# Five edits to the order and placement of work around a saturated TensorE in a two-layer retention and gMLP kernel

## The chip, the cores and the metric

The kernel runs on one core of a Trainium2 chip. A core has five engines that run side by side, each with its own instruction stream: TensorE (PE in the profile; PEld is its weight load), VectorE (DVE), ScalarE (ACT), GpSimd (POOL) and SyncE (SP). They work on tiles in on-chip memory (SBUF) and on the banks in which TensorE accumulates (PSUM); DMA queues, fed here by SP (loads, and the stores of the result) and by POOL (spills), move data to and from DRAM. The metric is the device time of one execution in microseconds.

## The reference

A latent stream x (512 tokens, 1024 features) and a context of 256 tokens pass through two layers, each behind an RMSNorm whose scale, shift and output gate come from a conditioning vector ("ada"), and then through a last RMSNorm. All is float32.

```
# layer 0: retention, 4 heads, q and k of 256, v of 512 features, both directions
q, k, v, z = split(h @ w_in)            # q and k with rotary positions
o = retention(q, k, v, log_g)           # scores (q k^T) times a decay matrix, times v; context first
o = o * rsqrt(mean(o * o) + eps)        # per token and head
x = x + gate * ((o * silu(z)) @ w_out)

# layer 1: gMLP, width 2048, 8 groups, chunks of 128 tokens
u, v, z = split(h @ w_in)
v = (v - mean(v)) * rsqrt(mean((v - mean(v))**2) + eps) * vnorm_g
mixed = einsum('gij,bnjgc->bnigc', w_s, v) + b_s
x = x + gate * ((u * mixed * silu(z)) @ w_out)
return rmsnorm(x, final_g)
```

## The kernel before, in words

**Products.** A float32 operand is split into a rounded high part and the rest (`split`: a cast on ScalarE, then a subtraction on VectorE), and each product is three matmuls (`mm3`). Big products are done as a scheme of seven half-size products in place of eight (`Product`, with the items B11, T1, T2, B21, T3, B22, T4 of one "quad"). For an item whose name begins with T, VectorE first subtracts two weight blocks (raw), then ScalarE casts and VectorE subtracts (hl), and TensorE runs 24 matmuls of 256 columns. The class `Stream` (its one instance is `Q`) holds the list of items and of weight loads; `Q.get` hands out an item's split tile and prepares two items ahead. Four hl buffers exist, and 11 small tiles ("t2") for everything of 128x512.

**Layer 0.** After the projections, `attend(h)` runs one head: twice three score steps (hf is the half of the 512 queries, j the pair of key blocks). A score step is 24 matmuls into a "tm" bank of PSUM, then pf (VectorE, times the decay), ph (cast, ScalarE) and pl (subtraction, VectorE). `pv`, two steps behind, multiplies by v into two "ps" banks. After the third pv of a half, `finish` norms it (ScalarE: squares into ss, a root, with a load of its function table; VectorE: reciprocal) and gates it (VectorE: two gt). `flip` transposes gt on TensorE and splits it into og. `project_out` multiplies by the output weights and adds to acc, the residual, which is loaded during head 0's scores. Beside the heads run the loads and splits of the next head's q, k (`load_qk`) and v, and in the background four "ada" pieces (bg) for the next layer's scale, shift and gate.

**Layer 1.** At the end of `project_out` of head 3, `rms(hf)` spreads the roots of a half's norm over the partitions with two tiny matmuls, into a bank of the pool "ps" (6 banks; "tm" has 2). v comes first (28 items): its blocks get their statistics (bn_stats) and are spilled to DRAM (vt). Then for i in 0 to 7, seven items of u and z; `load_vt` fetches v's block i+1 and normalises it; after B22 the spatial mix (16 small matmuls) follows, and `gate_f` gates two blocks of features: Silu on ScalarE, then on VectorE v times scale plus bias (ya, 128x512), times u (two of 128x256), times silu(z), and the split into y. Every second i, `out1(p)` multiplies four feature blocks by the output weights, in two halves hf of the columns; `drain` and `final` add up, norm and store.

**What sets the order.** Helper objects `pe`, `act`, `dve` (class `Queue`, line 54, so nearly all rows of the profile carry L54) issue the instructions. A scheduler places each engine's instructions by the program's text order and by what each waits for; `kept` pins an engine to the text order, `pinned` ties an instruction to the one before it, and `fence()` holds back all later ones of that engine until the one last issued. TensorE is kept throughout. Loads wait in SP's order, and a load waits for its slot (a tag such as "rope" or "w3") to come free.

Of the kernel before, what the change touches and what calls it, by code (L numbers as in the profile page):

```python
# [10 lines left out]
ALU = mybir.AluOpType  # L11
# [56 lines left out]
def hybrid_kernel(ctx, tc, xT_d, cT_d, cv_d, sv_d, rows_d, ada0_d, adag_d, w_d, rope_d, dec_d, ws_d, id_d, out_d):  # L68
# [181 lines left out]
    for q in QUADS[3:]:  # L250
        Q.quad(q, SINGLE)
        for u in RAWS:
            Q.load((q, u), W, 1, parts_of(q, u))
    PROJECTED = len(Q.items)
    def place_at(tag):
        return lambda: st([P, 2, 1024], tag, F32R, name="hl_e")
# [506 lines left out]
    def background():  # L763
        for i in range(4):
            a = None
            for a in ada_piece(i, *(("g1", ("g2", "g3")) if i < 3 else ("oA22", ("w2", "w3")))):
                if a is None:
                    yield
            yield
            if i == 0:  # L770
                yield from columns(a, gate0)
                dve.tensor_tensor(gate0, gate0, gateb0, ALU.add)
            elif i == 1:
                yield from columns(a, sh1)
                dve.tensor_tensor(sh1, sh1, adab1[:, 0, :], ALU.add)
                dve.tensor_tensor(shs, sh1[:, 0:4], sh1[:, 4:8], ALU.add)
            elif i == 2:
                yield from columns(a, gs1)
                dve.tensor_tensor(gs1, gs1, adab1[:, 1, :], ALU.add)
                dve.scalar_tensor_tensor(gs1, gs1, 1.0, g1, ALU.add, ALU.mult)  # L780
            else:
                gb = st([P, D], "g1", name="gateb1")
                load(gb, rows_d[0:1, :].partition_broadcast(P))
                yield
                for j in range(2):
                    pr = pt(tag="tm")
# [49 lines left out]
        dve.tensor_tensor(l, f32(l), f32(h), ALU.subtract)  # L836

    def load_qk(h):
        tags = ("s0", "s1", "s2", "s3", "rope") if h % 2 == 0 else ("w4", "w5", "g2", "g3", "w6")
        srcs = (k_d[h][0], q_d[h][0], k_d[h][1], kc_d[h], q_d[h][1])  # L840
        t = []
        for tag, src in zip(tags, srcs):
            t.append(st([P, 2, 2, HS], tag, F32R, name="qk"))
            load(f32(t[-1][:, 1]).rearrange("p a b -> p (a b)"), src)
            if len(t) % 2:
                yield
        for x in t:
            halves(x)
            yield
        qk[h] = (t[1], t[4]), (t[0], t[2]), t[3]  # L850
        yield
# [77 lines left out]
    def attend(h, qs, vs):  # L929
        q, k, kc = qk.pop(h)  # L930
        v, z = vv.pop(h)
        dt = dts[h]
        og = [st([P, 2, 4, HS], tag, F32R, name="og") for tag in ("oS3", "oS4")]
        steps = [(hf, j) for hf in range(2) for j in range(0, NK, 2)]
        ph, po, pend = {}, {}, []

        def key(j):
            return (k[j // 2], j % 2) if j < NT else (kc, j - NT)

        def score(hf, j):  # L940

            p = pt(tag="tm")
            for o in range(2):
                src, jj = key(j + 1 - o)
                for m in range(2):
                    l = (src[:, 0, m, jj * P:jj * P + P], src[:, 1, m, jj * P:jj * P + P])
                    mm3(p[:, o * HS:o * HS + HS], l, (q[hf][:, 0, m, :], q[hf][:, 1, m, :]), m == 0, m == 1)
            j1 = j + 1
            s0 = hf * HS - P * j1 + P * (NT - 1) if j < NT else XW + hf * HS - P * (j1 - NT) + P * (NC_T - 1)
            base = dt[:, s0:s0 + HS]  # L950
            both = bass.AP(base.tensor, base.offset, [base.ap[0], (P, 2), (1, HS)])
            two = lambda x: x.rearrange("p (o t) -> p o t", o=2)
            a = t2("pf")
            dve.scalar_tensor_tensor(two(a), two(p), 1.0 / 16.0, both, ALU.mult, ALU.mult)
            hl = t2("ph", dt=F32R), t2("pl", dt=F32R)
            split(hl, a)
            ph[hf, j] = hl

        def pv(hf, j):
# [12 lines left out]
        def finish(hf):  # L972
            ss = st([P, 2], "ss", bufs=2)
            for t in range(2):
                act.activation(t2("junk"), po[hf][t], AF.Square, accum_out=ss[:, t:t + 1])
            act.activation(ss, ss, AF.Sqrt, bias=eps, scale=1.0 / 512)
            dve.reciprocal(ss, ss)
            gts = []
            for t in range(2):
                g = t2("gt")  # L980
                dve.scalar_tensor_tensor(g, po[hf][t], ss[:, t:t + 1], z[:, 2 * hf + t, :], ALU.mult, ALU.mult)
                gts.append(g)
            pend.append((hf, gts))

        def flip():
            hf, gts = pend.pop(0)
            for fp in range(2):
                pq = pt()
                for b in range(2):
                    for t in range(2):  # L990
                        o = b * HS + t * P
                        pe.transpose(pq[:, o:o + P], gts[t][:, (2 * fp + b) * P:(2 * fp + b) * P + P], ident)
                src = pq.rearrange("p (b t) -> p b t", b=2)
                split((og[hf][:, 0, 2 * fp:2 * fp + 2, :], og[hf][:, 1, 2 * fp:2 * fp + 2, :]), src)

        LAG = 2
        wo = load_wo(h)
        for i in range(len(steps) + LAG):
            if i < len(steps):
                score(*steps[i])  # L1000
            if i >= LAG:
                pv(*steps[i - LAG])
            aside(qs)
            if i > 4:
                aside(vs)
            if i == len(steps):
                flip()
            if (h, i) == (0, 2):
                for c in range(4):
                    load(acc[:, 2 * c:2 * c + 2, :], xT_d[:, 2 * c:2 * c + 2, :])  # L1010
            if i < 5:
                aside(wo)
            if i in (3, 5, 6):
                step()
        return og, flip

    def project_out(ws, og, flip, parts, then=None, between=None, prepare=None):
# [72 lines left out]
        dve.reciprocal(s[:, 1, :], s[:, 1, :])  # L1090

    def rms(hf):
        pr = pt((P, HS))
        for i in range(2):
            mm(pr[:, i * P:i * P + P], sums[hf][:, 1, i:i + 1].to_broadcast([P, P]), ident, start=True, stop=True)
        rs = st([P, HS], "rs1", name="rs1")
# [114 lines left out]
    def out1(p):  # L1211
        for hf in range(2):
            ws = [Q.get() for _ in range(2)]
            pr = {}
            if p == 3 and hf == 0:
                seq = [(t, k) for ks in ((0, 1, 3), (2,)) for t in range(NT) for k in ks]
            else:
                seq = [(t, k) for t in range(NT) for k in range(4)]
            ends = (2,) if p == 3 and hf == 0 else (3,)
            for t, k in seq:  # L1220
                if k == 0:
                    pr[t] = pt()
                y = yf(4 * p + k)
# [1 line left out]
                mm3(pr[t], (y[:, 0, t * P:t * P + P], y[:, 1, t * P:t * P + P]), (w[:, 0, :], w[:, 1, :]), k == 0, k in ends)  # L1225
                if k in ends:
                    drain(p, t, hf, pr.pop(t))

    def drain(p, t, hf, pr):
        h = slice(hf * 512, hf * 512 + 512)  # L1230
# [15 lines left out]
    def final(t, hf, s, h):  # L1246
# [14 lines left out]
        act.activation(o[:, 512:], o[:, 512:], AF.Copy, scale=ss[:, 1:2])  # L1261
        load(rows[:, 512:], o[:, 512:])

    vts = {}

    def load_vt(i):
        vts[i] = []
        for th in range(2):
            v = t2("vt", (P, 2, HS))
            load(v, vt_d[i][:, 2 * th:2 * th + 2, :])  # L1270
            for t in range(2):
                n = 2 * th + t
                dve.tensor_scalar(v[:, t, :], v[:, t, :], mv[:, n, 0:1], rv[:, n:n + 1], ALU.subtract, ALU.mult)
            vts[i].append(v)

    def gate_f(f, pm, mine):

# [13 lines left out]
        split((y[:, 0, :], y[:, 1, :]), a)  # L1291

    load_vt(0)
    for i in range(UZ):
        got, pms = {}, {}
        prod = Product(features, got.__setitem__)
        for name in SINGLE:
            prod.run(name, Q.get())
            if name == "T2" and i < UZ - 1:
                load_vt(i + 1)  # L1300
            if name == "B22":
                for s in range(2):
                    pm = pms[s] = pt()
                    for n in range(NT):
                        mm(pm[:, n * P:n * P + P], vts[i][n // 2][:, n % 2, s * P:s * P + P], wsT[:, i * P:i * P + P], start=True, stop=True)
                gate_f(2 * i + 1, pms[1], {0: got["12"], 1: got["22"]})
        gate_f(2 * i, pms[0], {0: got["11"], 1: got["21"]})
        if i and i % 2 == 0:
            out1(i // 2 - 1)
    out1(3)  # L1310
# [110 lines left out]
```

## Time and profile before

| | us |
|---|---|
| median of three runs | 913.14 (909.51 to 913.16) |
| profiled execution | 911.76 |
| its span (first to last instruction) | 910.0 |
| busy: TensorE, VectorE, ScalarE | 886.6, 722.4, 445.5 |
| mean granted clock of TensorE | 0.997 |

How to read the rows: "start us, us, engine line op out<-in" is a group of instructions on one engine, xN their number; "[1.40 <-DVE pf L54]" says how long the engine stood idle ahead of it and which instruction ended the wait. Times count from the span's start. A row "PE pst L54 <- DVE hl L54: 3.7, 4, 1.6" gives the total of such waits, their number and the longest. In rows of groups, "| 11.5, 411 |" is the busy time in us and the mean length of one in ns. A window's row has the stretch, its length, and for each engine its busy time and number of instructions, then the clock granted to TensorE, the DMA share and GB/s.

### The profile page before, as it was taken

The numbers are of one execution on the slowest core, as the hardware profiler recorded it, in microseconds if no ns is written. First come the engines' busy times: TensorE is split into PE (matmuls) and PEld (weight loads), VectorE is DVE, ScalarE is ACT, GpSimd is POOL, SyncE is SP. The second block draws the span as 40 slices with busy tenths as digits, with TensorE's granted clock in tenths as the row PEclk, the third lists the DMA queues.
The fourth block names the chain that finished last, engine by engine and source line by source line (L and its number), as shares of the span: only waits on it lengthen the run. The fifth ranks groups of instructions, "written<-read, shape, count | busy, mean of one in ns | idle before, by whom it ended". The sixth has DMA issues, their size and how long they took to land.

```text
span 910.0 us, 16953 instructions
## 1 busy us (share of the span) xinstructions
PE 886.6 (97%) x6872; PEld 840.4 (92%) x6872; DVE 722.4 (79%) x1024; ACT 445.5 (49%) x683; POOL 51.5 (6%) x88
## 2 busy tenths in 40 slices
PE   8999999999999999999999999999999999999987
PEld 6899999999999998998989798999999899899885
DVE  3689978698789866888666759999899479679985
ACT  5565644434545436626362548744546445244244
POOL 0001211101102010000000001111000000000000
PEclk9999999999999999999999999999999999999999
DMA  9943968556667377758163611626335035037102
GB/s 334 389 136 111 308 200 255 163 183 223 211 207 241 107 254 251 257 164 282 43 194 107 200 37 66 200 102 220 129 116 185 24 116 185 24 117 253 49 24 93
DMA packets 76782, 153.81 MB, mean 169 GB/s; under 512 B 7840, under 2 KB 34592, under 8 KB 76704
## 3 DMA queue, kind: packets, MB, share of 16 engines
q1 hardware_dynamic: 69840, 130.70, 44.5%
q0 software_dynamic: 6720, 22.03, 6.3%
q8 instruction: 54, 0.88, 0.4%
q14 instruction: 24, 0.20, 0.1%
q10 hardware_dynamic: 144, 0.01, 0.0%
HBM read 128.58 MB, written 24.12 MB: 168 GB/s over the span
## 4 chain that ended last, share of the span: by engine, by line
PE 61%; DVE 20%; DMA 7%; ACT 5%; issue 5%; SPq 1%; DVEq 0%; ACTq 0%
PE pst L54 61%; DVE hl L54 5%; DMA raw<-in_w_dram 4%; DVE raw L54 4%; DVE ya L54 2%; ACT hl L54 2%; DVE o L54 2%; DMA vt<-vt 2%; SPq L128 1%; DMA acc<-in_xT_dram 1%; DVE pf L54 1%; DMA xq<-in_xT_dram 1%; DVE snap L54 1%; DVE ada_a L54 1%; ACT junk L54 1%
## 5 line engine op out<-in xcount | busy, mean ns | idle before, releaser
L54 DVE TENSOR_TENSOR hl<-raw,hl 128x1024 fp32r<-128x1024 f32 x195 | 236.7, 1222 | 65.5 <-ACT hl L54 64.8
L54 ACT CAST hl<-raw 128x1024 fp32r<-128x1024 f32 x195 | 202.7, 1049 | 140.9 <-DVE raw L54 71.1
L54 PE MATMUL pst<-oS,hl 128*128 128x256 f32 x1104 | 135.6, 280 | 4.3 <-DVE hl L54 3.7
L54 PEld LDWEIGHTS pst<-oS,hl 128*128 128x128 f32 x1104 | 131.4, 188 | 6.6 <-ACT ya L54 3.6
L54 PE MATMUL pst<-hl,oS 128*128 128x256 f32 x1152 | 137.3, 279 | 0.1
L54 PEld LDWEIGHTS pst<-hl,oS 128*128 128x128 f32 x1152 | 135.6, 188 | 1.2 <-ACT snap L54 0.8
L54 PE MATMUL pst<-oA,hl 128*128 128x256 f32 x936 | 118.1, 281 | 0.2
L54 PEld LDWEIGHTS pst<-oA,hl 128*128 128x128 f32 x936 | 112.6, 188 | 2.6 <-DVE raw L54 0.8
L54 DVE TENSOR_TENSOR raw<-raw 128x1024 f32<-128x1024 f32 x92 | 111.5, 1221 | 0.8
L54 PE MATMUL pst<-hl,oA 128*128 128x256 f32 x816 | 99.4, 280 | 0.1
L54 ACT COPY snap<-pst 128x512 f32<-128x512 f32 x92 | 53.9, 586 | 89.4 <-PE pst L54 89.1
L54 PEld LDWEIGHTS pst<-hl,oA 128*128 128x128 f32 x816 | 96.9, 188 | 0.4 <-issue 0.3
L54 PE MATMUL pst<-og,hl 128*128 128x256 f32 x768 | 93.1, 281 | 0.0
L54 PEld LDWEIGHTS pst<-og,hl 128*128 128x128 f32 x768 | 91.2, 188 | 1.0 <-issue 0.5
L54 PE MATMUL pst<-hl,ya 128*128 128x512 f32 x288 | 69.6, 394 | 2.4 <-DVE ya L54 2.4
L54 PEld LDWEIGHTS pst<-hl,ya 128*128 128x128 f32 x288 | 53.9, 188 | 14.7 <-DVE ya L54 2.9
L54 PE MATMUL pst<-v,ph 128*128 128x512 f32 x192 | 60.9, 399 | 0.0
L54 DVE TENSOR_TENSOR snap<-pst,snap 128x512 f32<-128x512 f32 x69 | 47.4, 687 | 4.1 <-PE pst L54 3.9
L54 ACT CAST ph<-pf 128x512 fp32r<-128x512 f32 x24 | 14.9, 621 | 70.9 <-DVE pf L54 68.5
L54 PE MATMUL pst<-hl,hc 128*128 128x256 f32 x384 | 47.5, 279 | 0.0
L54 PEld LDWEIGHTS pst<-hl,hc 128*128 128x128 f32 x384 | 45.9, 188 | 0.0
L54 PEld LDWEIGHTS pst<-v,ph 128*128 128x128 f32 x192 | 36.7, 191 | 7.7
(172 smaller groups left out, 971.8 us busy)
## 6 DMA issues: line engine op xcount, KB each, us to landing
raw<-in_w_dram SPq DMA_DIRECT2D x224, 256.0 KB, 4.5
bg<-in_adag_dram SPq DMA_DIRECT2D x32, 512.0 KB, 4.4
ada_w<-in_ada_dram SPq DMA_DIRECT2D x16, 512.0 KB, 9.0
raw<-in_w_dram SPq DMA_DIRECT2D x16, 512.0 KB, 4.4
bg<-in_dec_dram SPq DMA_DIRECT2D x12, 512.0 KB, 4.3
v<-snap POOLq DMA_DIRECT2D x16, 256.0 KB, 5.1
z<-snap POOLq DMA_DIRECT2D x16, 256.0 KB, 4.7
v<-v SPq DMA_DIRECT2D x8, 512.0 KB, 4.2
```

The lines of the kernel that those rows point to most:

```text
L54: made = op(*args, **kw)
L128: nc.sync.dma_start(dst, src)
```

## The change

1. **q slot.** The last q tile of heads 0 and 2 is loaded into slot "w3" in place of "rope"; the last projection quad leaves "w3" out of its slots, and ada piece 3 uses "rope" in its place.
2. **Gating and last scores.** `finish` ends with the root. Reciprocal and gt move to `gated()`, called after the next score step (and at the loop's end); after the split of the last score step ScalarE and VectorE get a fence.
3. **Spread roots.** `rms` takes a "tm" bank.
4. **v.** `load_vt` only loads (after T1, was T2); `norm_vt` (after T4) normalises by ScalarE, as Identity with bias -mean times root and scale root.
5. **Gating in layer 1.** `gate_f` is put in a list `owed` and issued by `settle()` after the next `Q.get`, behind a fence on VectorE.
6. **The last product.** `out1(3)` for the first half takes features 0 and 1 of all token tiles, then 3, then 2; the last token tile of the second half is done in two halves of 256 columns, each drained by `last`, and the last store is issued from ScalarE's queue.

```diff
-            Q.load((q, u), W, 1, parts_of(q, u))
+            Q.load((q, u), W if q != QUADS[-1] else [w for w in W if w != "w3"], 1, parts_of(q, u))
...
-            for a in ada_piece(i, *(("g1", ("g2", "g3")) if i < 3 else ("oA22", ("w2", "w3")))):
+            for a in ada_piece(i, *(("g1", ("g2", "g3")) if i < 3 else ("oA22", ("w2", "rope")))):
...
-        tags = ("s0", "s1", "s2", "s3", "rope") if h % 2 == 0 else ("w4", "w5", "g2", "g3", "w6")
+        tags = ("s0", "s1", "s2", "s3", "w3") if h % 2 == 0 else ("w4", "w5", "g2", "g3", "w6")
...
             split(hl, a)
+            if (hf, j) == steps[-1]:
+                act.fence()
+                dve.fence()
...
             act.activation(ss, ss, AF.Sqrt, bias=eps, scale=1.0 / 512)
-            dve.reciprocal(ss, ss)
...
+            rest.append((hf, ss))
+
+        def gated():
+            while rest:
+                hf, ss = rest.pop(0)
+                dve.reciprocal(ss, ss)
...
                 score(*steps[i])
+            gated()
             if i >= LAG:
                 pv(*steps[i - LAG])
...
-        pr = pt((P, HS))
+        pr = pt((P, HS), tag="tm")
...
             ws = [Q.get() for _ in range(2)]
             pr = {}
+            settle()
             if p == 3 and hf == 0:
-                seq = [(t, k) for ks in ((0, 1, 3), (2,)) for t in range(NT) for k in ks]
+                seq = [(t, k) for ks in ((0, 1), (3,), (2,)) for t in range(NT) for k in ks]
...
+            if (p, hf) == (3, 1):
+                t = NT - 1
+                for c in range(2):
+                    pq = pt((P, HS))
+                    for k in range(4):
...
+                        mm3(pq, (y[:, 0, t * P:t * P + P], y[:, 1, t * P:t * P + P]), (w[:, 0, :], w[:, 1, :]), k == 0, k == 3)
+                    last(t, c, pq)
...
+    def last(t, c, pq):
+
+        h = slice(512 + c * HS, 512 + c * HS + HS)
+        s = o1[t][:, h]
+        dve.tensor_tensor(s, pq, s, ALU.add)
+        ss, o = ends[t]
+        act.activation(t2("junk1", (P, HS)), s, AF.Square, accum_out=ss[:, 1:2])
+        dve.tensor_tensor(o[:, h], s, fg[:, h], ALU.mult)
+        if c == 0:
+            dve.scalar_tensor_tensor(ss[:, 0:1], ss[:, 1:2], 1.0 / D, ss[:, 0:1], ALU.mult, ALU.add)
+            return
...
+        nc.scalar.dma_start(rows[:, 512:], o[:, 512:])
...
-            for t in range(2):
-                n = 2 * th + t
-                dve.tensor_scalar(v[:, t, :], v[:, t, :], mv[:, n, 0:1], rv[:, n:n + 1], ALU.subtract, ALU.mult)
             vts[i].append(v)
+
+    nb = st([P, NT], "nb")
+    dve.scalar_tensor_tensor(nb, mv[:, :, 0], -1.0, rv, ALU.mult, ALU.mult)
+
+    def norm_vt(i):
+        for n in range(NT):
+            v = vts[i][n // 2][:, n % 2, :]
+            act.activation(v, v, AF.Identity, bias=nb[:, n:n + 1], scale=rv[:, n:n + 1])
+
+    owed = []
+
+    def settle():
+        if owed:
+            dve.fence()
+        while owed:
+            owed.pop(0)()
...
-            prod.run(name, Q.get())
-            if name == "T2" and i < UZ - 1:
-                load_vt(i + 1)
+            w = Q.get()
+            settle()
+            prod.run(name, w)
+            if i < UZ - 1:
+                if name == "T1":
+                    load_vt(i + 1)
+                if name == "T4":
+                    norm_vt(i + 1)
...
-                gate_f(2 * i + 1, pms[1], {0: got["12"], 1: got["22"]})
-        gate_f(2 * i, pms[0], {0: got["11"], 1: got["21"]})
+                owed.append(lambda f=2 * i + 1, pm=pms[1], mine={0: got["12"], 1: got["22"]}: gate_f(f, pm, mine))
+        owed.append(lambda f=2 * i, pm=pms[0], mine={0: got["11"], 1: got["21"]}: gate_f(f, pm, mine))
+        if i == UZ - 1:
+            settle()
```

What this does to the engines' instructions, at three places.

On SP, at the end of layer 0's projections and the start of head 0 (qk<-q_156 is head 0's last q tile, bg the first raw block of an ada piece, acc the residual):

```order
 L128 DMA qk<-k_165 128x512
-L128 DMA bg<-in_adag_dram 128x1024
+L128 DMA qk<-q_156 128x512
 L128 DMA v<-v_175 128x1024
 L128 DMA bg<-in_dec_dram 128x1024
```

```order
 L128 DMA raw<-in_w_dram 128x1024
-L128 DMA acc<-in_xT_dram 128x1024
-L128 DMA qk<-q_156 128x512
-L128 DMA acc<-in_xT_dram 128x1024 x3
+L128 DMA acc<-in_xT_dram 128x1024 x4
+L128 DMA bg<-in_adag_dram 128x1024
```

The q tile has moved up, out of the residual's loads, and the bg block has moved down behind them.

On VectorE, around the last score step of the first half of head 3 (hl_e is the first split of layer 1, raw a weight difference for it, og the split behind the flip):

```order
 L54 TENSOR_TENSOR pl<-pf,ph 128x512
+L54 SCALAR_TENSOR_TENSOR pf<-pst,dt 128x512
+L54 TENSOR_TENSOR hl<-raw,hl 128x1024
+L54 TENSOR_TENSOR pl<-pf,ph 128x512
+L54 RECIPROCAL ss<-ss 128x2
 L54 TENSOR_TENSOR hl_e<-raw,hl_e 128x1024
-L54 TENSOR_TENSOR raw<-raw 128x1024 x2
-L54 RECIPROCAL ss<-ss 128x2
 L54 SCALAR_TENSOR_TENSOR gt<-pst,ss,z 128x512 x2
-L54 TENSOR_TENSOR hl<-raw,hl 128x1024
-L54 SCALAR_TENSOR_TENSOR pf<-pst,dt 128x512
-L54 TENSOR_TENSOR pl<-pf,ph 128x512
```

The last pf and pl, and the split hl between them, have moved ahead of the gating, and one of the two raw that stood ahead of it now follows the next og.

On VectorE in layer 1, where the blocks of u1 are gated while the items of u2 are prepared. Before:

```order
L54 TENSOR_TENSOR raw<-raw 128x1024 x2
L54 TENSOR_TENSOR snap<-pst,snap 128x512
L54 TENSOR_TENSOR hl<-raw,hl 128x1024
L54 SCALAR_TENSOR_TENSOR ya<-pst,sv,bsb 128x512 x2
L54 TENSOR_TENSOR ya<-snap,ya 128x256 x3
L54 TENSOR_TENSOR ya<-ya,yz 128x512
L54 TENSOR_TENSOR ya<-pst,ya 128x256
L54 TENSOR_TENSOR raw<-raw 128x1024
L54 TENSOR_TENSOR ya<-ya 128x512
L54 TENSOR_TENSOR ya<-ya,yz 128x512
L54 TENSOR_TENSOR hl<-raw,hl 128x1024
```

Now:

```order
L54 TENSOR_TENSOR snap<-pst,snap 128x512
L54 TENSOR_TENSOR raw<-raw 128x1024
L54 SCALAR_TENSOR_TENSOR ya<-pst,sv,bsb 128x512
L54 TENSOR_TENSOR ya<-snap,ya 128x256 x2
L54 TENSOR_TENSOR hl<-raw,hl 128x1024
L54 TENSOR_TENSOR ya<-ya,yz 128x512
L54 SCALAR_TENSOR_TENSOR ya<-pst,sv,bsb 128x512
L54 TENSOR_TENSOR hl<-raw,hl 128x1024
L54 TENSOR_TENSOR ya<-ya 128x512
L54 TENSOR_TENSOR ya<-snap,ya 128x256
L54 TENSOR_TENSOR ya<-pst,ya 128x256
```

Before, the split of item T2 (the last hl above) came behind both gates; now it comes behind the first three instructions of one, and the next split behind two more.

More of the change, by code (lines that the diff above doesn't have):

```diff
@@ L934, in attend @@
         steps = [(hf, j) for hf in range(2) for j in range(0, NK, 2)]
-        ph, po, pend = {}, {}, []
+        ph, po, pend, rest = {}, {}, [], []
         def key(j):
@@ L976, in finish @@
             act.activation(ss, ss, AF.Sqrt, bias=eps, scale=1.0 / 512)
-            dve.reciprocal(ss, ss)
-            gts = []
-            for t in range(2):
[L980 to L983, printed above, removed]
+            rest.append((hf, ss))
[3 more added lines that the diff above has]
+                dve.reciprocal(ss, ss)
+                gts = []
+                for t in range(2):
+                    g = t2("gt")
+                    dve.scalar_tensor_tensor(g, po[hf][t], ss[:, t:t + 1], z[:, 2 * hf + t, :], ALU.mult, ALU.mult)
+                    gts.append(g)
+                pend.append((hf, gts))
         def flip():
@@ L1014, in attend @@
                 step()
+        gated()
         return og, flip
@@ L1220, in out1 @@
             for t, k in seq:
+                if (p, hf, t) == (3, 1, NT - 1):
+                    continue
                 if k == 0:
@@ L1227, in out1 @@
                     drain(p, t, hf, pr.pop(t))
+            if (p, hf) == (3, 1):
[3 more added lines that the diff above has]
+                    for k in range(4):
+                        y = yf(4 * p + k)
+                        o = k % 2 * 512 + c * HS
+                        w = ws[k // 2][:, :, o:o + HS]
+                        mm3(pq, (y[:, 0, t * P:t * P + P], y[:, 1, t * P:t * P + P]), (w[:, 0, :], w[:, 1, :]), k == 0, k == 3)
+                    last(t, c, pq)
     def drain(p, t, hf, pr):
@@ L1262, in final @@
         load(rows[:, 512:], o[:, 512:])
+    def last(t, c, pq):
[8 more added lines that the diff above has]
+            return
+        rows = out_d[t * P:t * P + P, :]
+        act.activation(ss[:, 1:2], ss[:, 1:2], AF.Sqrt, bias=ss[:, 0:1], scale=1.0 / D)
+        dve.reciprocal(ss[:, 1:2], ss[:, 1:2])
+        dve.tensor_scalar(o[:, 0:512], o[:, 0:512], ss[:, 1:2], None, ALU.mult)
+        load(rows[:, 0:512], o[:, 0:512])
+        act.activation(o[:, 512:], o[:, 512:], AF.Copy, scale=ss[:, 1:2])
+        nc.scalar.dma_start(rows[:, 512:], o[:, 512:])
     vts = {}
@@ L1270, in load_vt @@
             load(v, vt_d[i][:, 2 * th:2 * th + 2, :])
-            for t in range(2):
-                n = 2 * th + t
-                dve.tensor_scalar(v[:, t, :], v[:, t, :], mv[:, n, 0:1], rv[:, n:n + 1], ALU.subtract, ALU.mult)
             vts[i].append(v)
+    nb = st([P, NT], "nb")
[10 more added lines that the diff above has]
+            owed.pop(0)()
     def gate_f(f, pm, mine):
@@ L1293, in hybrid_kernel @@
     load_vt(0)
+    norm_vt(0)
     for i in range(UZ):
```

## Prediction

> **What bounds the kernel.** I read the page's busy table first, then the waits of TensorE, then the rows around each wait.
>
> ```profile
> span 910.0 us, 16953 instructions
> PE 886.6 (97%) x6872; PEld 840.4 (92%) x6872; DVE 722.4 (79%) x1024; ACT 445.5 (49%) x683; POOL 51.5 (6%) x88
> PE pst L54 <- DVE hl L54: 3.7, 4, 1.6
> PE pst L54 <- DVE pl L54: 3.1, 2, 2.1
> PE pst L54 <- DVE ya L54: 2.4, 1, 2.4
> PE pst L54 <- DVE pf L54: 1.4, 1, 1.4
> PE pst L54 <- ACT xs L54: 1.2, 1, 1.2
> ```
>
> TensorE is busy for 886.6 of 910.0 us, so at most 23.4 us can be won without removing matmuls, and this change removes none. The waits (us in total, times, longest) that it touches add up to 3.7 + 3.1 + 2.4 + 1.4 + 1.2 = 11.8 us in nine places. Everything else is startup, the store at the end, or small. So the sum goes place by place, and what VectorE or ScalarE gain elsewhere counts for nothing.
>
> A wait costs a little more than its idle time, because the end of the last matmul before it is modelled:
>
> ```profile
> 878.84 1.56 PE L54 MATMUL pst<-hl,ya 128*128 128x512 f32 x6
> 882.83 3.48 PE L54 MATMUL pst<-hl,ya 128*128 128x512 f32 x14 [2.43 <-DVE ya L54]
> 882.08 1.29 DVE L54 TENSOR_TENSOR ya<-ya 128x512 fp32r<-128x512 f32 x2
> ```
>
> Fourteen take 3.48 us and six 1.56, so one more costs 1.92/8 = 0.24. The six from 878.84 would let the next start at 880.28; it starts at 882.83, and 2.55 us are lost where 2.43 are shown. I add 0.13 to each wait.
>
> **The change, part by part.**
>
> **The q slot.** Head 0's scores begin late:
>
> ```profile
> 306.68 0.33 SPq L128 DMA_DIRECT2D bg<-in_adag_dram  x1
> 335.78 0.33 SPq L128 DMA_DIRECT2D qk<-q  x1
> 343.49 0.62 ACT L54 CAST qk<-qk 128x512 fp32r<-128x512 f32 x1 [3.54 <-DMA qk<-q]
> 346.75 0.69 DVE L54 SCALAR_TENSOR_TENSOR pf<-pst,dt 128x512 f32<-128x512 f32 x1
> 347.49 1.68 PE L54 MATMUL pst<-qk 128*128 128x256 f32 x12 [1.40 <-DVE pf L54]
> ```
>
> ScalarE stands 3.54 us for the last q tile, issued on SP's queue at 335.78 between the residual (acc) loads; the v splits queue behind it, and the first pf ends at 347.44. In the order of after, this load stands in the place of the bg load of 306.68, some 29 us earlier, and its cast and subtraction lie inside the projection. ScalarE's 3.54 us go; pf then starts some 2 us earlier and TensorE no longer waits: **-1.5 us** (1.40 + 0.13). The bg load moves behind the four acc loads; its reader is background work off TensorE's path. Bounds: 0, if v's splits come as late as before, and -1.8.
>
> **Gating behind the last scores.** Today VectorE gates first, then does pf and pl of the last score step; now the gating (reciprocal and two gt, 0.16 + 1.41 us by rows below) stands behind pl. So the last score-times-v product (pv) no longer waits for pl, but the transposes (flip) ahead of it wait for gt.
>
> ```profile
> 367.76 0.69 DVE L54 TENSOR_TENSOR pl<-pf,ph 128x512 fp32r<-128x512 f32 x1 [0.69 <-ACT ph L54]
> 367.36 1.03 PE L54 MATMUL pst<-ident,gt 128*128 128x128 f32 x8
> 368.50 0.50 PE L54 MATMUL pst<-v,pl 128*128 128x512 f32 x1
> 418.88 0.50 PE L54 MATMUL pst<-v,pl 128*128 128x512 f32 x1 [0.95 <-DVE pl L54]
> ```
>
> In heads 0 to 2 VectorE does the same pieces in another order; the one saving is the 0.69 us that it stands for ph, now filled by splits. The chain that ended with pl at 368.45 now ends with gt at 367.76; the flip takes 1.03 us more, so pv starts at about 368.8 against 368.50. Head 1 goes the same way (from 418.88 to 419.2). I take **+1.05 us** for the three; bounds 0 (all splits hidden earlier) and +3 (nothing filled, and the flip exposed each time).
>
> Head 3 is different:
>
> ```profile
> 512.45 1.05 ACT L54 CAST hl_e<-raw 128x1024 fp32r<-128x1024 f32 x1 [1.44 <-DMA raw<-in_w_dram]
> 513.40 0.59 ACT L54 ACTIVATE junk<-pst 128x512 f32<-128x512 f32 x1
> 516.17 1.03 ACT L54 CAST hl<-raw 128x1024 fp32r<-128x1024 f32 x1
> 511.58 1.57 PE L54 MATMUL pst<-qk 128*128 128x256 f32 x12
> 517.38 1.41 DVE L54 SCALAR_TENSOR_TENSOR gt<-pst,ss,z 128x512 f32<-128x512 f32 x2
> 518.49 1.34 PE L54 MATMUL pst<-ident,gt 128*128 128x128 f32 x8
> 521.96 0.50 PE L54 MATMUL pst<-v,pl 128*128 128x512 f32 x1 [2.12 <-DVE pl L54]
> 522.00:526.00 4.00, 4.00 (x12) 0.64 0.40 130
> ```
>
> Layer 1's first split (hl_e) waits 1.44 us for a load, and the squares for the norm queue behind it on ScalarE; the new fence puts hl_e behind ph. The stretch from the squares to the end of hl's cast (513.40 to 517.20) can then start where the pv ahead of the last scores (511.58) ends, at about 511.2: hl's cast ends at 515.0, ph's (0.6) at 515.6, hl's subtraction (1.22) at 516.2, and pl (0.69) at 516.9. Reciprocal (0.16), hl_e's subtraction (1.23) and gt (1.41) bring 519.5 with their overlaps, the flip (1.0) 520.5, against 521.96: **-1.5 us**. And from 518.49 to 521.96, 3.47 us, TensorE did transposes only; in the window behind it (its columns: length, PE busy, granted clock, DMA share, GB/s) the clock is 0.64, which costs 4.00 x 0.36 = 1.4 us. The new stretch is 2.0 us. After the 2.43 us wait at 882.83 matmuls go at their full 0.24 us, so I take the drop as gone: **-1.4 us**; bounds -1.4 and 0.
>
> The Trainium skill ("TensorE: Matmul & The Clock Gate", Part 1) has the clock halved after an idle window of about 3.4 us that runs freely, and (Part 4) does not count transposes as activity. The rows put the limit between 2.43 and 3.47 us, which agrees; by its figure the sum would stay as it is, but its "HAM oscillation" speaks against a change that adds short waits around transposes: see the third rival.
>
> **The bank of the spread roots.**
>
> ```profile
> 560.20 0.16 DVE L54 RECIPROCAL sums<-sums 128x2 f32<-128x2 f32 x1
> 561.80 0.71 PE L54 MATMUL pst<-ident,sums 128*128 128x128 f32 x4 [1.16 <-ACT xs L54]
> 550.00:600.00 50.00, 48.60 (x408) 47.96 (x409) 49.27 (x71) 37.67 (x63) 6.46 (x12) 1.00 0.44 148
> ```
>
> The roots are ready at 560.36, but TensorE waits until 561.80 for ScalarE to free a "ps" bank (xs). With a "tm" bank it waits for the roots only: 1.16 + 0.13 less some 0.1 gives **-1.2 us**. VectorE is busy for 49.27 of these 50 us, so the time may come back as a wait for hl: bounds -1.5 and 0.
>
> **v normalised by ScalarE, gating deferred.** The four waits for hl all lie in layer 1. The longest:
>
> ```profile
> DVE vt L54 <- DMA vt<-vt: 11.0, 10, 2.0
> L54 DVE TENSOR_SCALAR vt<-vt,mv,rv 128x256 f32<-128x256 f32 x32 | 11.5, 411 | 11.1 <-DMA vt<-vt 11.0
> L54 ACT ACTIVATE f<-f,sh,gs 128x256 f32<-128x256 f32 x16 | 8.3, 592 | 1.1 <-DVE f L54 1.1
> 679.06 1.22 DVE L54 TENSOR_TENSOR hl<-raw,hl 128x1024 fp32r<-128x1024 f32 x1
> 685.84 1.23 DVE L54 TENSOR_TENSOR hl<-raw,hl 128x1024 fp32r<-128x1024 f32 x1
> 682.63 2.99 PE L54 MATMUL pst<-oS,hl 128*128 128x256 f32 x24
> 687.21 1.06 PE L54 MATMUL pst<-oS,hl 128*128 128x256 f32 x7 [1.60 <-DVE hl L54]
> ```
>
> TensorE wants the next item at about 685.5, when the 24 matmuls end; VectorE turns to its subtraction at 685.84, having done both gates since 680.2. In the new order raw comes first (1.22), then one gate's first three pieces (some 1.5), then hl (1.22): ready at about 684.0 at the latest, 1.5 us ahead, and 1.4 us more are free where vt's four instructions stood, so the splits behind it move up too. The four waits go: 3.7 + 4 x 0.13 = **-4.3 us**. VectorE loses 11.5 us of work and 11.0 of waiting; ScalarE gains 32 instructions, like its 128x256 Identity at 0.59 us 19 us, and is busy for 49%. These lie beside TensorE's items; with the cover gone they would cost what the split behind them is late. Bounds -4.3 and 0.
>
> **The last gating and product.** Before, tile 0 uses features 0, 1 and then 3, whose y ends at 882.7 (the first ya of 882.08). Now features 0 and 1 of all four token tiles come first, 24 x 0.24 = 5.8 us: feature 3 is wanted at 884.6, and the wait goes: **-2.55 us**. Next is feature 2, wanted 12 matmuls later (887.5), ready at 883.4 already in before.
>
> ```profile
> 898.73 4.97 PE L54 MATMUL pst<-hl,ya 128*128 128x512 f32 x21
> 900.29 6.78 SPq L128 DMA_DIRECT2D out_dram<-o  x8
> ```
>
> Cutting the last block in two halves costs TensorE nothing (24 x 0.12 = 12 x 0.24). Behind the last matmul (903.70) an add and a square are half as wide, at most -0.6 us, and the last store leaves from ScalarE's queue, for which the trace has no row: from 0 to the 0.33 us that SP's issues take, either way. I take **-0.3 us**.
>
> **The sum**: -1.5 + 1.05 - 1.5 - 1.4 - 1.2 - 4.3 - 2.55 - 0.3 = **-11.7 us**. The profiled execution took 911.76 us, so 900.1; it lies 1.38 under the median of the runs shown (913.14), from which the sum gives 901.4. I forecast **900.7**.
>
> **Rivals.**
>
> 1. **The flip takes the waits over**: gt ends as late as pl did in every head, and the busy VectorE gives the 561.80 wait back as one for hl. Then heads 0 to 2 cost 3 x 1.0, head 3 and its clock stay, the bank brings 0: -1.5 + 3.0 - 4.3 - 2.55 - 0.3 = -5.65, 906.1. For it: VectorE's 49.27 of 50. Against: the 0.69 us that it stands for ph.
> 2. **Layer 1's waits stay under another name**: ScalarE, with 19 us more and the loads of vt ahead of its casts, is late where VectorE was. Then -4.3 drops out: 904.4. That the change doesn't do what it says has the same price; the order of after speaks against it. Both rivals together: 910.4.
> 3. **The clock drops at the new waits too**, as it did behind 518.49, with transposes and waits adding up: 1.4 us in each of the four heads, -11.7 + 4 x 1.4 = -6.1, 905.7. Against: 882.83 and its 0.24 us. [...]
> 4. **Slower: ScalarE stands for vt.** The loads now wait for tiles that the deferred gates free, and a snap and two casts queue behind them.
>
> ```profile
> DMA to landing us min/median/max: 2.3/4.2/6.5
> ```
>
> The splits run two items ahead: 2 x 2.8 us less the 2.3 that a split takes is 3.3 us of cover. If each of seven loads lands 6.5 us after ScalarE has come to it, 7 x 3.2 = 22.4 us are lost: 922.5. It reverses the sign from 5.0 us late (3.3 + 11.7/7). VectorE's longest wait for vt was 2.0.
>
> **Chances.** Forecast 0.53, first rival 0.14, second 0.14, both 0.09, third 0.05, fourth 0.05. By 0.5% (4.6 us, about what a measurement here can tell from no change): faster 0.86, same 0.09, slower 0.05. The range goes from 896 (heads 0 to 2 without loss and the last tenths, 898.3, less the 2.25 us by which the fastest run lies under the profiled one) to 907.5 (the first rival, with the 1.4 us up to the median).
>
> **What would show it.** Right: no rows of TensorE waiting for pf at 347, for xs at 561, for ya at 882, none for hl over 0.3 us in layer 1, a clock of 1.00 behind head 3's last pv, and short new waits for gt (0.3 to 1.1 us). Wrong: a wait for gt over 1.5 us in any head, rows of ScalarE waiting for vt over 3 us, or new waits for hl from 565 to 640.

## The result, and the profile after

| | before | after |
|---|---|---|
| median (range, runs) in us | 913.14 (909.51 to 913.85, 5) | 899.1 (898.68 to 899.66, 5) |
| ratio, 95% interval | | 0.9847, 0.9825 to 0.987 |
| span of the profiled execution | 910.0 | 897.0 |

The kernel became 1.5% faster: 14.0 us between the medians, 13.0 between the two profiled spans. The forecast was 900.7 us, in a range from 896 to 907.5.

The busy table and the waits of TensorE after (us in total, times, longest):

```profile
span 897.0 us, 16978 instructions
PE 883.0 (98%) x6884; PEld 839.4 (94%) x6884; DVE 715.7 (80%) x996; ACT 459.9 (51%) x717; POOL 51.5 (6%) x88
```

```profile
PE pst L54 <- DVE gt L54: 1.5, 5, 0.5
PE pst L54 <- DVE snap L54: 0.7, 1, 0.7
PE pst L54 <- DVE hl L54: 0.7, 2, 0.4
```

Of the five waits that the sum was made of, those for pl, ya, pf and xs have no row any more, and hl's fell from 3.7 to 0.7. New are gt, as forecast, and snap (and 0.4 us for junk at 9 us, in the startup). TensorE's rows at those places:

```profile
343.01 4.36 PE L54 MATMUL pst<-qk 128*128 128x256 f32 x36
347.21 0.39 PE L54 MATMUL pst<-v,pl 128*128 128x512 f32 x1
415.47 0.33 PE L54 MATMUL pst<-ident,gt 128*128 128x128 f32 x1 [0.48 <-DVE gt L54]
416.12 0.98 PE L54 MATMUL pst<-ident,gt 128*128 128x128 f32 x7 [0.33 <-DVE gt L54]
516.84 0.33 PE L54 MATMUL pst<-ident,gt 128*128 128x128 f32 x1
517.49 0.98 PE L54 MATMUL pst<-ident,gt 128*128 128x128 f32 x7 [0.33 <-DVE gt L54]
518.23 0.47 PE L54 MATMUL pst<-v,pl 128*128 128x512 f32 x1
584.55 3.18 PE L54 MATMUL pst<-hl,oA 128*128 128x256 f32 x25 [0.74 <-DVE snap L54]
587.99 0.74 PE L54 MATMUL pst<-hl,oA 128*128 128x256 f32 x4 [0.26 <-DVE hl L54]
852.54 0.73 PE L54 MATMUL pst<-oS,hl 128*128 128x256 f32 x4 [0.39 <-DVE hl L54]
```

The 36 score matmuls of head 0 now run in one piece into the first pv. The flip of head 1 waits for each of the two gt, that of head 3 for the second, and pv follows at once. At 584.55, 587.99 and 852.54 stand waits that before did not have. The windows (length, busy time of five engines, granted clock, DMA share, GB/s) behind head 3's flip and at the roots:

```profile
518.20:522.20 4.00, 4.00 (x25) 3.50 (x24) 2.79 (x4) 2.58 (x7) 0.00 (x0) 1.00 0.09 32
550.00:600.00 50.00, 49.00 (x416) 48.58 (x415) 49.12 (x66) 34.96 (x55) 6.46 (x12) 1.00 0.44 148
```

The clock behind head 3 is 1.00 where it was 0.64. VectorE is still busy for 49 of the 50 us around the roots.

Since TensorE's order is nearly unchanged, the start of one and the same matmul in both traces shows where the time went:

| the matmul | before | after | shift | step |
|---|---|---|---|---|
| first pv of head 0 | 349.23 | 347.21 | -2.02 | q slot -2.0 |
| pv behind head 2's flip | 470.10 | 468.17 | -1.93 | gating, heads 0 to 2: +0.1 |
| first of head 3's output product | 526.29 | 521.07 | -5.22 | head 3 and its clock: -3.3 |
| roots of the second half | 561.80 | 555.10 | -6.70 | bank -1.3, rest -0.1 |
| first spatial mix | 652.53 | 647.19 | -5.34 | given back: +1.4 |
| last spatial mix | 874.26 | 863.84 | -10.42 | gMLP: -5.1 |
| last matmul | 903.32 | 890.74 | -12.58 | last gating and product: -2.2 |
| end of the span | 910.0 | 897.0 | -13.0 | drain and last store: -0.4 |

The profiled execution of gate_at_once below took 2382 us, so its trace isn't read and its time comes from the other five.

### The profile page after: what moved, and what is told of

Read it like the earlier page. It is cut to its first block, busy times and chain, and to the rows that moved or that the text cites. A ratio compares the mean times of both kernels' runs of the same rounds, so it can differ in the third digit from the quotient of the medians.

```text
span 897.0 us, 16978 instructions
## 1 busy us (share of the span) xinstructions
PE 883.0 (98%) x6884; PEld 839.4 (94%) x6884; DVE 715.7 (80%) x996; ACT 459.9 (51%) x717; POOL 51.5 (6%) x88
## 4 chain that ended last, share of the span: by engine, by line
PE 75%; DVE 13%; ACT 6%; issue 3%; DMA 2%; SPq 1%; ACTq 0%; DVEq 0%
PE pst L54 75%; DVE hl L54 3%; DVE o L54 2%; ACT hl L54 2%; DVE ada_a L54 1%; DVE raw L54 1%; ACT junk L54 1%; DMA xq<-in_xT_dram 1%; DMA bg<-in_dec_dram 1%; ACT L54 1%; DVE pl L54 1%; DVE gt L54 1%; DVE pf L54 1%; DVE ya L54 1%; DVE f L54 1%
## 5 line engine op out<-in xcount | busy, mean ns | idle before, releaser
L54 PE MATMUL pst<-hl,ya 128*128 128x512 f32 (+1 forms) x300 | 69.3, 384 | 0.0
```

Of the source, the lines that this page charges most:

```text
L54: made = op(*args, **kw)
```

## The experiments

Times are compared with the runs of before on the same chip (ratio with its interval), and with the changed kernel's 899.1 us (898.68 to 899.66).

### Layer 1: which part of the gMLP edit removed the waits for hl

The edit has three parts: v on ScalarE, v's load a product earlier and its use later in the program text (T1 and T4 in place of T2 and T2), and the deferred gating. The first two runs each undo one part.

```diff
# gate_at_once (changed kernel)
-                owed.append(lambda f=2 * i + 1, pm=pms[1], mine={0: got["12"], 1: got["22"]}: gate_f(f, pm, mine))
+                gate_f(2 * i + 1, pms[1], {0: got["12"], 1: got["22"]})
-        owed.append(lambda f=2 * i, pm=pms[0], mine={0: got["11"], 1: got["21"]}: gate_f(f, pm, mine))
-        if i == UZ - 1:
-            settle()
+        gate_f(2 * i, pms[0], {0: got["11"], 1: got["21"]})
```

> The changed kernel with the deferral undone: gate_f is issued at once, without the fence; v stays on ScalarE. Theory (the deferral is what removes the waits for hl in layer 1): TensorE waits 3 to 4 us for hl again between 640 and 860 in about four places, 902 to 903.5 in all. Rival (taking v off VectorE is enough): under 0.7 us of such waits, 899 to 900.

Measured: 899.01 us, ratio 0.9845 (0.9822 to 0.9868). The theory, that the deferral does it, falls.

```diff
# v_on_dve (changed kernel)
-            act.activation(v, v, AF.Identity, bias=nb[:, n:n + 1], scale=rv[:, n:n + 1])
+            dve.tensor_scalar(v, v, mv[:, n, 0:1], rv[:, n:n + 1], ALU.subtract, ALU.mult)
```

> The changed kernel with v normalised by VectorE again, at the same place in the text; the deferral stays. Theory (the deferral alone does most): under 1.5 us of new waits of TensorE, 899 to 900.6. Rival (VectorE's free time is what lets the splits come in time): 3 to 5 us of waits for hl come back, 902 to 904.

Measured: 898.94 us, 0.9848 (0.9825 to 0.987). So v's place on ScalarE isn't needed either. In this trace VectorE has no wait for vt at all, though it normalises v as in before, where it stood 11.0 us for it. That gave a new theory: the part left over, the new places of v's load and use, does it. Two runs test it on the changed kernel: both_undone takes both edits above together, and de_undone also puts load and use back behind T2.

```diff
# de_undone = both_undone, and
-                if name == "T1":
-                    load_vt(i + 1)
-                if name == "T4":
-                    norm_vt(i + 1)
+                if name == "T2":
+                    load_vt(i + 1)
+                    norm_vt(i + 1)
```

> The changed kernel with the deferral undone and v on VectorE, but with v's loads still issued after T1 and used after T4. New theory (the waits for hl came from VectorE standing 11.0 us for loads of v that it had just asked for, and the earlier load alone cures it): VectorE waits under 1 us for vt, TensorE under 1 us for hl in layer 1, 898.5 to 900. Rival (either the deferral or ScalarE is needed, each standing in for the other): 2.5 to 4.5 us of waits for hl, 901.5 to 903.5.

> The changed kernel with the whole gMLP edit undone: v on VectorE, loaded and used after T2, gating at once; the new order of features in the last product stays. New theory: the four waits for hl are back (3.7 us shown, 4.3 in time), VectorE stands 9 to 12 us for vt, and the last gating is still hidden by the order of features: 902.7 to 904. Rival (the waits went for another reason, say the order on SP): under 1.5 us of waits, 899 to 900.5.

Measured: both_undone 898.35 us, 0.984 (0.9814 to 0.9866); de_undone 903.91 us, 0.9895 (0.9871 to 0.992). The waits of TensorE for hl and of VectorE for vt, first both_undone, then de_undone:

```profile
PE pst L54 <- DVE hl L54: 0.3, 1, 0.3
DVE vt L54 <- DMA vt<-vt: 4.8, 2, 2.6
```

```profile
PE pst L54 <- DVE hl L54: 3.0, 5, 1.1
DVE vt L54 <- DMA vt<-vt: 10.4, 10, 1.7
```

With load and use back in the old places the waits are back (one of the five, 0.3 us, is the one near 588); with the new places alone they are gone, and VectorE's two remaining waits for vt, up to 2.6 us, cost TensorE nothing. The expectation of under 1 us for vt was wrong there, that for TensorE right. Last, the same part alone on the kernel before:

```diff
# v_place (kernel before)
-            if name == "T2" and i < UZ - 1:
-                load_vt(i + 1)
+            if i < UZ - 1:
+                if name == "T1":
+                    load_vt(i + 1)
+                if name == "T4":
+                    norm_vt(i + 1)
```

(load_vt now only loads; norm_vt holds the old four VectorE instructions.)

> The kernel before with one edit: v's block is loaded after T1 and normalised after T4, still by VectorE. Theory (this alone removes the waits for hl in layer 1): TensorE waits under 0.8 us for hl there, still about 2.4 us for ya at the last gating, 3 to 4.5 us faster than before. Rival (in the kernel before the gates' place matters too): 2 us or more of waits for hl stay, under 2.5 us faster.

Measured: 907.14 us, 0.9948 (0.9927 to 0.997), which is 4.7 us with an interval from 2.7 to 6.7. TensorE's waits:

```profile
PE pst L54 <- DVE pl L54: 2.9, 2, 2.1
PE pst L54 <- DVE pf L54: 2.5, 1, 2.5
PE pst L54 <- DVE ya L54: 2.2, 1, 2.2
PE pst L54 <- ACT xs L54: 1.2, 1, 1.2
```

The row for hl is gone, all others of before are there. The new places of load and use are sufficient. What they do is seen on SP and VectorE at v's third block, in before and then in v_place (TensorE is equally far in both: its next spatial mix begins at 675.18 and 675.02):

```profile
667.97 0.85 SPq L128 DMA_DIRECT2D vt<-vt  x2
671.69 0.74 DVE L54 TENSOR_SCALAR vt<-vt,mv,rv 128x256 f32<-128x256 f32 x2 [0.71 <-DMA vt<-vt]
```

```profile
658.25 1.12 SPq L128 DMA_DIRECT2D vt<-vt  x2
667.11 1.37 DVE L54 TENSOR_SCALAR vt<-vt,mv,rv 128x256 f32<-128x256 f32 x4
```

The load is asked for 8.9 us ahead of its use in place of 3.7, and lands in time. The use isn't later but 4.6 us earlier, though it is later in the text: the scheduler moved both. No run has the earlier load without the other place of the use, so which of the two halves is needed stays open.

### The last gating

```diff
# y_order (changed kernel)
-                seq = [(t, k) for ks in ((0, 1), (3,), (2,)) for t in range(NT) for k in ks]
+                seq = [(t, k) for ks in ((0, 1, 3), (2,)) for t in range(NT) for k in ks]
```

> The changed kernel with features 0, 1, 3 of the last product in the old order. Theory of the prediction (the order of features wins the 2.55 us): a wait for ya of 2 to 2.6 us, 901 to 902. Rival (the deferral already finishes feature 3 at 869.5 in the changed kernel, and it is wanted at 869.8, so the order is a second cover of the same wait): a wait under 0.3 us, 898.7 to 899.6.

Measured: 899.67 us (898.45 to 900.4), 0.9853 (0.9823 to 0.9884). The start of the last product on TensorE, and the split of feature 3 on VectorE:

```profile
869.44 2.73 PE L54 MATMUL pst<-hl,ya 128*128 128x512 f32 x11
869.86 0.69 DVE L54 TENSOR_TENSOR ya<-ya 128x512 fp32r<-128x512 f32 x1 [0.69 <-ACT ya L54]
```

Feature 3 is ready at 870.55, before the seventh matmul (869.44 + 6 x 0.23 = 870.8) wants it. The rival was right: with the deferral, the order of features covers nothing. And de_undone, which has the order of features but not the deferral, shows no wait for ya either: each of the two edits is enough, and 2.55 us are there once.

### The bank of the roots

```diff
# bank_ps (changed kernel); bank_only (kernel before) is the reverse
-        pr = pt((P, HS), tag="tm")
+        pr = pt((P, HS))
```

> The changed kernel with one edit undone: the spread roots use a ps bank again. Theory (what the bank wins at the roots comes back 25 us later, as waits for snap and hl, because the scheduler lets the earlier roots pull VectorE's scaling ahead and push weight differences back): TensorE waits about 1.2 us for xs at the roots, the waits for snap (0.7) and hl (0.3) near 585 are gone, and the time is within 0.7 us of the changed kernel's 899.1. Rival (the bank is worth its 1.2 us and the waits near 585 have another cause): both kinds of wait are there and the time is about 900.4.

> The kernel before with the bank edit alone. Theory (most of the bank's win is returned 25 us later): the wait for xs (1.2 us) goes, new waits for snap and hl of 0.8 to 1.1 us come near 590, and the time falls by 0 to 0.6 us, which cannot be told from none. Rival (the returned waits need the other edits): no new waits near 590, 1.2 to 1.5 us faster.

Measured: bank_ps 900.5 us (899.95 to 900.92), 0.9866 (0.9846 to 0.9886); bank_only 912.55 us, 1.0003 (0.9982 to 1.0023). In bank_ps the wait is back at the roots:

```profile
PE pst L54 <- ACT xs L54: 1.2, 1, 1.2
```

and snap falls to 0.2 us in all. In bank_only the wait for xs is gone, and 29 us behind the roots stand the same two waits as in the changed kernel:

```profile
591.40 3.16 PE L54 MATMUL pst<-hl,oA 128*128 128x256 f32 x25 [0.75 <-DVE snap L54]
594.84 1.44 PE L54 MATMUL pst<-hl,oA 128*128 128x256 f32 x10 [0.28 <-DVE hl L54]
```

So the bank edit alone brings them. With it the scheduler has the roots earlier, puts VectorE's scaling by them ahead of two weight differences (raw, 1.22 us each) and ahead of a snap, and those come late (the two raw stand at 579.66 and 584.32 in the changed kernel; before has none between 565 and 590). By the starts in the traces it wins 1.3 us at the roots and has given back 0.8 (bank_ps against the changed kernel) to 1.0 (bank_only against before) by the first spatial mix. bank_ps was expected within 0.7 us and is 1.4 above; by its trace 1.1 us of that were already there at head 1's flip, far ahead of the edit, in a stretch that varies between executions (its gt wait was 0.87 us here and 0.48 in the changed kernel's trace, with the same instructions). A further 0.4 us is the slower pitch of its first output product (last section). How much of the 1.4 us belongs to the bank isn't settled; by the starts in the traces the bank nets 0.3 to 0.5.

### Gating in the heads

```diff
# no_fence (changed kernel)
-            if (hf, j) == steps[-1]:
-                act.fence()
-                dve.fence()
# gating_first = no_fence, reciprocal and gt back in finish(), and
-            gated()
             if i >= LAG:
```

> The changed kernel with the order of gating and last scores undone and without the two fences. Theory (nearly all of this edit's gain is head 3, wait and clock; heads 0 to 2 are a draw): head 3's last product waits about 2.1 us for pl, the granted clock behind it falls to about 0.64, heads 0 to 2 differ by under 0.5 us in all, 902.0 to 902.8 in all. Rival (the clock and the wait went because of work elsewhere): no drop of the clock, under 1 us of difference, about 899.5.

> The changed kernel without the two fences behind the last score step; gating still comes after the scores. Theory (in head 3 the fence does it, by holding layer 1's first split, which waits for a load, behind ph): head 3's flip or pv waits 2 to 3.5 us, the other heads as in the changed kernel, 901 to 902.8. Rival (the order of gating alone does it): head 3 within 0.6 us of the changed kernel, 899 to 899.8.

Measured: gating_first 900.92 us (898.79 to 903.26), 0.9872 (0.9851 to 0.9893); no_fence 901.28 us (898.98 to 902.18), 0.987 (0.9838 to 0.9902). gating_first at head 3's flip on TensorE, and the window behind it:

```profile
517.25 1.39 PE L54 MATMUL pst<-ident,gt 128*128 128x128 f32 x8
520.76 0.50 PE L54 MATMUL pst<-v,pl 128*128 128x512 f32 x1 [2.12 <-DVE pl L54]
```

```profile
520.70:524.70 4.00, 3.94 (x22) 3.42 (x22) 1.21 (x3) 1.80 (x6) 0.00 (x0) 1.00 0.41 131
```

The wait of 2.1 us is back, as expected, but the clock behind it stays at 1.00, though the stretch without products is 3.51 us, as long as in before. So the expected time was 1 to 2 us too high, and this order doesn't bring the drop each time (the last section says when). Without the fences, head 3 on ScalarE and TensorE:

```profile
510.62 1.05 ACT L54 CAST hl_e<-raw 128x1024 fp32r<-128x1024 f32 x1 [1.45 <-DMA raw<-in_w_dram]
518.44 0.33 PE L54 MATMUL pst<-ident,gt 128*128 128x128 f32 x1 [1.68 <-DVE gt L54]
520.34 0.78 PE L54 MATMUL pst<-v,pl 128*128 128x512 f32 x1
```

hl_e is again ahead of the squares and waits 1.45 us for its load, and the flip waits 1.68 us for gt. pv starts 2.1 us later than in the changed kernel (518.23), while heads 0 to 2 stay as they were. So head 3 needs the fence; the moved gating without it only moves the wait from pv to the flip. The fence without the moved gating was not run.

### The q slot

```diff
# q_only (kernel before)
-            Q.load((q, u), W, 1, parts_of(q, u))
+            Q.load((q, u), W if q != QUADS[-1] else [w for w in W if w != "w3"], 1, parts_of(q, u))
...
-            for a in ada_piece(i, *(("g1", ("g2", "g3")) if i < 3 else ("oA22", ("w2", "w3")))):
+            for a in ada_piece(i, *(("g1", ("g2", "g3")) if i < 3 else ("oA22", ("w2", "rope")))):
...
-        tags = ("s0", "s1", "s2", "s3", "rope") if h % 2 == 0 else ("w4", "w5", "g2", "g3", "w6")
+        tags = ("s0", "s1", "s2", "s3", "w3") if h % 2 == 0 else ("w4", "w5", "g2", "g3", "w6")
```

> The kernel before with the q slot alone. Theory: the wait for pf at head 0's scores (1.4 us in the profiled execution of before) goes, nothing takes its place, and the time falls by 1.5 to 3.5 us, more than the profile says where the load lands later in other executions. Rival (the bg load, now behind the residual, or v's splits are late in its place): under 0.7 us.

Measured: 908.95 us, 0.9962 (0.9941 to 0.9982), that is 3.5 us with an interval from 1.6 to 5.4. The wait for pf is gone. The profile of before understates it: in other executions with the old slot pf was later, 2.5 us in v_place above and 3.54 in bank_only, both with a drop of the clock behind it.

### A version that beats both

Since the waits for gt are what the heads have left, gates_early starts from both_undone and moves the two splits that stand between the last pf and its pl (of the next head's q or k, and of an output weight) behind the gating:

```diff
# gates_early (both_undone)
             gated()
+            if i == 5:
+                aside(qs)
+                aside(wo)
             if i >= LAG:
                 pv(*steps[i - LAG])
-            aside(qs)
+            if i != 4:
+                aside(qs)
...
-            if i < 5:
+            if i < 4:
                 aside(wo)
```

> The kernel both_undone (898.35) with one more edit: in attend, the splits of the next head's q and k and of the output weights that stood between pf and pl of the last score step come behind the gating, so ph, pl, the reciprocal and gt follow pf directly. Theory (the waits for gt, 1.7 us shown in five places, are made of those two casts and subtractions): waits for gt under 0.5 us, 895.8 to 897.2. Rival (the splits moved are themselves wanted soon): new waits for pl, hl or qk eat it, 898 or more.

Measured: 895.49 us (894.14 to 896.51, 6 runs), ratio to before 0.9812 (0.9784 to 0.984), and 3.6 us under the changed kernel, with no overlap of the runs (the intervals of the two ratios do overlap a little; the spans of the profiled executions are 892.9, 897.0 and, for both_undone, 895.7). The flips of heads 1 and 3 and the pv behind them:

```profile
414.18 1.03 PE L54 MATMUL pst<-ident,gt 128*128 128x128 f32 x8
414.98 0.48 PE L54 MATMUL pst<-v,pl 128*128 128x512 f32 x1
514.70 1.04 PE L54 MATMUL pst<-ident,gt 128*128 128x128 f32 x8
515.49 0.48 PE L54 MATMUL pst<-v,pl 128*128 128x512 f32 x1
```

No row waits for gt any more; eight transposes and pv follow without a gap.

## Why the prediction was right, point by point

**What bounds the kernel**: right. The time came from TensorE's waits and its clock alone; VectorE's busy share did not fall (79% to 80%).

**The q slot**: right mechanism, -1.5 forecast, -2.0 in the trace. In the runs it is worth 3.5 us, probably because the profiled execution of before had one of the shorter waits. The size of a wait for a load was taken from one execution.

**Gating in heads 0 to 2**: +1.05 forecast, +0.1 by the starts of the matmuls (the shift goes from -2.02 to -1.93); the direction within the heads, a flip that waits for gt and a pv that doesn't wait for pl, was right. **Head 3**: -1.5 - 1.4 = -2.9 forecast, -3.3 measured, and no_fence shows that it needs the fence on hl_e, as the step said. About 1.4 us of it is the drop that the profiled execution of before happened to have.

**The clock**: the step "the rows put the limit between 2.43 and 3.47 us" failed. The drop is gone in the changed kernel, but gating_first has a stretch of 3.51 us with none and bank_only one of 2.34 us with one: what counts is how busy TensorE is in windows that lie fixed in time (last section). Transposes count there, where the prediction cites the Trainium skill ("TensorE: Matmul & The Clock Gate", Part 4) for the opposite: the measurement decides. The third rival, drops at the new short waits, did not come.

**The bank**: the step "a 'tm' bank gives -1.2" failed in its net. The roots gained their 1.3 us, and 1.4 came back by the first mix in the changed kernel, of which the two bank runs put 0.8 to 1.0 down to the bank; what gave back the rest was not looked for. The bound of 0 was nearer than the 1.2, and the reason given for it (a busy VectorE gives the time back as a wait) holds in bank_only. One sign of being wrong that the prediction named, new waits for hl from 565 to 640, did show, at 587.99. The order of after had shown the moved weight differences; the step counted them as work saved ahead of an item, and not as work that comes later in a full engine.

**v and the deferral**: -4.3 forecast (3.7 + 4 x 0.13 is 4.2), -5.1 measured, but the reason failed. The step said that the splits come in time because the gates follow them and because v's four instructions are gone. gate_at_once, v_on_dve, both_undone and v_place show that neither is needed: VectorE was late because it stood for loads of v that had been asked for too late. The row that said so, VectorE's 11.0 us for vt, was quoted and counted as a side gain. Whether gating later or ScalarE would have removed the waits with v's load in its old place was not run. The deferral comes with a cost, the 0.39 us wait at 852.54, which both_undone does not have; it is over the 0.3 us that the prediction allowed for hl in layer 1. Of the 5.1 us, 0.8 are a faster pitch of two products, which may be luck: the same instructions can run at either pitch in two executions (last section).

**The last gating**: -2.55 forecast; the wait is gone, but not because of the order of features: y_order shows that the deferral had covered it already. The last product ran at a slower pitch than before, 0.4 us in all, so 2.2 came out. **Drain and store**: -0.3 forecast, -0.4 measured.

**The sum** of -11.7 came out as -13.0 in the spans and -14.0 in the medians. In the spans the terms were too small by 0.5 for the q slot, 0.95 for heads 0 to 2, 0.4 for head 3, 0.8 for the gMLP and 0.1 for the drain, and too large by 1.2 for the bank and 0.35 for the last product: that the sum came so near is in part luck. The further 1.0 us in the medians comes from the profiled execution of before, which was a quick one (911.76 against a median of 913.14).

## What to carry to other kernels

Where an in-order engine waits for a load which it has just asked for, the late result shows up at another engine, several instructions on; look for that row before the work behind it is rearranged, since an earlier request may be all that is needed. When a bundle of edits removes a wait, undo each alone and all together: here the wait for ya was covered twice, so undoing one cover showed nothing, and two of three parts of the gMLP edit turned out not to be needed. A resource that comes free earlier also moves a scheduler's choices in a full engine; look at the order behind the place, not only at the place.

## What the runs showed of the hardware that was not expected

**The clock follows how busy TensorE was in fixed windows of 3.41 us.** The length of a gap does not decide: in the traces of all these kernels, behind the startup, no stretch under 2.3 us without products had a drop behind it, and of sixteen between 2.3 and 3.8 us seven had one. In bank_only, stretches of 3.70 us (head 0) and 2.34 us (last gating) had one and 3.12 us (head 3) had none. The clock records of the traces say why. Every change of the granted clock lies a whole number of 3.413 us behind its first rise; in bank_only one drop ends at 354.18 and the next begins at 883.25, and 529.07 us are 155 x 3.413. A low stretch lasts one such window or two. Here are three of these windows, each with the one behind it, two from bank_only and then one from q_only (length, TensorE's busy time, granted clock, DMA share, GB/s):

```profile
521.43:524.85 3.42, 1.52 (x11) 1.00 0.08 29
524.85:528.26 3.41, 3.22 (x16) 1.00 0.46 154
879.83:883.25 3.42, 1.24 (x6) 1.00 0.01 2
883.25:886.66 3.41, 3.41 (x10) 0.50 0.00 0
```

```profile
516.80:520.21 3.41, 1.48 (x11) 1.00 0.15 41
520.21:523.62 3.41, 3.41 (x10) 0.50 0.43 132
```

The thirteen traces that can be read hold some 3400 such windows up to the last matmul. Twelve were followed by a low clock: TensorE had been busy in them for 0.56 to 1.48 us, if time at half clock counts half (in q_only 2.59 us at half clock count as 1.30, and that drop went on for a second window). All others, with 1.51 us or more, were followed by the full clock, gating_first's 3.51 us stretch among them with 1.66. Transposes count: of the 1.52 us at 521.43, 1.04 are transposes, and by products alone that window would lie far below the 1.24 at 879.83. So whether a gap brings a drop hangs on where it falls in these windows, and that differs between executions: the first rise lies 3.9 to 7.0 us behind the span's start. The Trainium skill ("TensorE: Matmul & The Clock Gate", Part 1) gives an idle window of about 3.4 us that runs freely; the traces agree with the length (3.413 us) and the free run, but the window need not be idle. This rule was read off the traces afterwards, and no run was made to test it.

By it an execution like the changed kernel's profiled one can't have a drop: behind the startup TensorE is busy for at least 2.6 us of any 3.41, wherever they begin (its longest stretch without products is 2.04 us). In before this goes down to 1.2 us behind head 3's last scores and 1.0 at the last gating, and chance decides. A low window costs up to 1.7 us, half of its length. This fits the scatter: the 17 runs of before on one chip (908.38 to 917.22 us) have mean granted clocks from 0.992 to 0.999, and the lower clock goes with the longer time (correlation -0.81); the changed kernel's five (898.68 to 899.66) all have 0.998 or 0.999.

**Products of 512 columns run at one of two pitches.** In the third output product, before and then after:

```profile
840.49 1.56 PE L54 MATMUL pst<-hl,ya 128*128 128x512 f32 x6
843.29 1.56 PE L54 MATMUL pst<-hl,ya 128*128 128x512 f32 x6
```

```profile
829.90 1.54 PE L54 MATMUL pst<-hl,ya 128*128 128x512 f32 x6
832.65 1.54 PE L54 MATMUL pst<-hl,ya 128*128 128x512 f32 x6
```

From row to row lie 12 matmuls: 2.80/12 = 0.233 us before, 2.75/12 = 0.229 after, at a granted clock of 1.00 in both. Each product of 96 keeps one of the two all through; before has the fast one in the first and fourth, after in the first three. One product is 0.4 us longer or shorter by it. It is not set by the order of instructions alone: in the first product the changed kernel has 0.229 and y_order, whose edit touches only the last product, 0.233. What sets it stays open.
